# Gated DeltaNet layer: block inverses of two heads side by side, split weight buffers, last two scans in parallel

## The chip, the cores and the metric

The kernel runs on one NeuronCore of a Trainium2 chip. The metric is device time in microseconds (us) of one execution, the median of several runs. One execution is taken by the hardware profiler; its trace and page are what is quoted. Engines: PE is TensorE's matmul and PEld its weight load, DVE is VectorE, ACT is ScalarE, POOL is GpSimd, SP is SyncE, which issues the DMAs.

## The reference

A trunk of two pre-norm layers on 512 tokens of width 1024, float32: a gated DeltaNet layer, a squared-ReLU MLP (hidden width 4096), an HGRN2 layer, a second MLP and a last RMSNorm. The change lies in the first layer. With 8 heads of 128 and chunks, for each head:

```python
L = jnp.where(strict, jnp.einsum('nbhik,nbhjk->nbhij', kb, k) * decay, 0.0)
sol = lax.linalg.triangular_solve(L, rhs, left_side=True, lower=True, unit_diagonal=True)
...
def step(S, xs):
    v_new = u_c - jnp.einsum('bhck,bhkv->bhcv', w_c, S)
    o = jnp.einsum('bhck,bhkv->bhcv', qd, S) + jnp.einsum('bhij,bhjv->bhiv', a_c, v_new)
    S = S * dl[..., None, None] + jnp.einsum('bhck,bhcv->bhkv', kd, v_new)
```

The triangular system of each chunk is solved for every head; the recurrence over chunks (the scan) is then serial within a head. The head's output is normalised, multiplied by a gate and projected.

## The kernel before, in words

Activations lie with features on the 128 partitions and the 512 tokens along the free axis. Every projection in full precision is made of three products of rounded parts: a weight tile of 1024 x 256 is loaded as `raw` (L105), split into a high part `whi` by ScalarE (L111) and a low part `wlo` by VectorE (L112), each in two halves, and `project` (L122 to L124) issues for each of the 8 input blocks high x high, high x low and low x high, 128x512 each. A tile is a pair of 128-wide output blocks, 48 such products. `raw` has two buffers, `whi` and `wlo` three each.

In the DeltaNet layer (`gdn`, L269) a loop runs over j = 0 to 9. In step j the inputs of head j+1 are projected and convolved (`gdn_conv`), and, at a raised priority, the scan of head j-2 (`gdn_scan`), the local part of head j (`gdn_local`) and the block inverse of head j-1 (`gdn_inverse`) are issued; gate projections stand in steps 4, 6, 8 and 9 (`GATES`). The kernel uses chunks of 128 tokens, four in a head. A scheduler makes from the priorities and from the buffers one fixed order for each engine; the projections of later heads, of the gates and of the output projection fill TensorE between the small steps.

`gdn_inverse` inverts the four 128x128 unit triangular matrices of a head. It starts from 32x32 diagonal blocks, four blocks in each of four matrices, 16 products in a group, placed on the four diagonal 32x32 tiles of the array. For each of four levels:

- a group px (L499), ScalarE copies it to xd (L502);
- a group pu (L506), VectorE copies it into ud under a mask (L508) and transposes ud into wd (L509).

Then the 32-blocks are joined to 64 (px L516, pu L524 and L525) and the 64-blocks to 128 (px L536, pu L540). GpSimd copies ud to the diagonal of the result u (L511, four copies) and wd into w2 (L530, two copies), the operand of the 64x64 step. A float32 product runs in two passes, so a group of 16 products shows as x32 in the trace. A head has 12 such groups.

`gdn_scan` runs over the four chunks: pks (L559), r on VectorE, pw (L564), wv on VectorE, ps (L569), the new state s on VectorE, with the output po (L576, L578) beside it. The result is scaled by ScalarE into ot (L585, L591), transposed (pt, L594) and goes to VectorE. Then the gate is multiplied in and split into oh and ol, the inputs of the output projection (`out_proj`, L825), which starts with two weight tiles at once and goes through the heads in order; products with early heads stand on TensorE while the last scan runs.

PSUM: three buffers for projections, two with tag "ma" (local part and scan), three with tag "mb" (inverse).

Of the kernel before, what the change touches and what calls it, by code (L numbers as in the profile page):

```python
# [26 lines left out]
LINE, PAD = 2048, 352  # L27
LEVELS = (1, 2, 4, 8, 16)
HLEVELS = (2, 4, 8, 16, 32)
GATES = ((), (), (), (), (0,), (), (1,), (), (2,), (3,))  # L30


class Net:
    def __init__(self, tc, ctx, a):
        self.tc, self.nc, self.a = tc, tc.nc, a
        pool = lambda name, bufs=1, **kw: ctx.enter_context(tc.tile_pool(name=name, bufs=bufs, **kw))

        self.cp = pool("const")
        self.mp = pool("small")
# [6 lines left out]
        self.n = 0  # L46
        self.last_switch, self.since_switch = None, []
# [221 lines left out]
    def gdn(self, first):  # L269
# [23 lines left out]

        self.o, self.on = [None] * NH, [None] * NH
        hd = {0: self.gdn_conv(0, blocks)}
        self.gdn_silu([hd[0]])
        for j in range(NH + 2):
            todo = []
            if j + 1 < NH:
                hd[j + 1] = self.gdn_conv(j + 1, blocks)  # L300
                todo.append(hd[j + 1])
            sg = []
            for i in GATES[j]:
                sg += self.gdn_gates(i)
            with self.tc.high_priority(offset=3000):
                if j >= 2:
                    self.gdn_scan(j - 2, hd)
                if j < NH:
                    self.gdn_local(j, hd)
                if 1 <= j <= NH:  # L310
                    self.gdn_inverse(j - 1, hd)
                if todo or sg:
                    self.gdn_silu(todo, sg)
            for h, t in sg:
                self.gdn_gated(h, t)
        self.h = [self.load_x(c) for c in range(NB)]

# [54 lines left out]
    def gdn_conv(self, j, blocks):  # L372
        nc = self.nc
        kq = self.work("kq", [P, 2, T], bufs=4)
        v = self.work("v", bufs=4)
# [36 lines left out]
    def gdn_local(self, h, hd):  # L412
# [8 lines left out]
        ssk, ssq = self.work("ssk", [P, NC]), self.work("ssq", [P, NC], bufs=3)  # L421
        kd, e = self.work("kd", bufs=3), self.work("e")
# [13 lines left out]
        dd = self.work("dd", [P, NC], bufs=3)  # L436
# [23 lines left out]
        n, aa = self.work("n", bufs=2), self.work("aa", bufs=3)  # L460
# [14 lines left out]
    def gdn_inverse(self, h, hd):  # L475


        nc, mm, ident = self.nc, self.nc.tensor.matmul, self.ident
        n = hd[h][5].rearrange("p (c t) -> p c t", c=NC)
        blk = [slice(b, b + B) for b in range(0, P, B)]  # L480
        small = lambda name, bufs=1: self.work(name, [P, NC, B], bufs=bufs)
        psum = lambda name: self.mix(name, [P, NC, B], tag="mb")
        flat = lambda t: t.rearrange("p c t -> p (c t)")
        mask = lambda i: self.lmask[:, i].unsqueeze(1).to_broadcast([P, NC, B])
        uw = self.work("uw", [P, 2, T], bufs=2)
        u = uw[:, 0].rearrange("p (c t) -> p c t", c=NC)
        nc.gpsimd.memset(uw[:, 0], 0.0)
        ud, wd = small("ud"), small("wd")
        nc.gpsimd.tensor_copy(out=wd, in_=self.ident32.unsqueeze(1).to_broadcast([P, NC, B]))
        nt = small("xd")  # L490
        for b in blk:
            nc.vector.transpose(out=nt[b], in_=n[b, :, b])
        nc.vector.copy_predicated(out=wd, mask=mask(0), data=nt)
        nc.vector.transpose(out=flat(ud), in_=flat(wd))
        for i in range(1, len(LEVELS)):
            px = psum("px")
            for c in range(NC):
                for b in blk:
                    mm(px[b, c], lhsT=n[b, c, b], rhs=wd[b, c], start=True, stop=True,  # L499
                       tile_position=(b.start, b.start))  # L500
            x = small("xd")
            nc.scalar.copy(out=x, in_=px)  # L502
            pu = psum("pu")
            for c in range(NC):
                for b in blk:
                    mm(pu[b, c], lhsT=x[b, c], rhs=ud[b, c], start=True, stop=True,  # L506
                       tile_position=(b.start, b.start))
            nc.vector.copy_predicated(out=ud, mask=mask(i), data=pu)  # L508
            nc.vector.transpose(out=flat(wd), in_=flat(ud))  # L509
        for b in blk:  # L510
            nc.gpsimd.tensor_copy(out=u[b, :, b], in_=ud[b])  # L511

        px, x = psum("px"), small("xd")
        for c in range(NC):
            for l, r in (blk[0:2], blk[2:4]):
                mm(px[r, c], lhsT=n[l, c, r], rhs=wd[l, c], start=True, stop=True, tile_position=(l.start, r.start))  # L516
# [3 lines left out]
        l, r = blk[0], blk[1]  # L520
        w2 = uw[:, 1, 0:2 * B * NC].rearrange("p (c t) -> p c t", c=NC)
        for c in range(NC):
            for l, r in (blk[0:2], blk[2:4]):
                mm(pu[l, c], lhsT=x[r, c], rhs=ud[r, c], start=True, stop=True, tile_position=(r.start, l.start))  # L524
            mm(pu[blk[1], c], lhsT=ud[blk[1], c], rhs=x[blk[1], c], start=True, stop=True, tile_position=(B, B))  # L525
        for l, r in (blk[0:2], blk[2:4]):
            nc.vector.tensor_copy(out=u[l, :, r], in_=pu[l])
        nc.gpsimd.memset(w2[0:B, :, B:2 * B], 0.0)
        for i in (0, 1):
            nc.gpsimd.tensor_copy(out=w2[blk[i], :, i * B:(i + 1) * B], in_=wd[blk[i]])  # L530
        nc.vector.tensor_copy(out=w2[blk[1], :, 0:B], in_=pu[blk[1]])

        l, r = slice(0, 64), slice(64, P)
        px = self.mix("px", [P, NC, 2 * B], tag="mb")
        for c in range(NC):
            mm(px[r, c], lhsT=n[l, c, r], rhs=w2[l, c], start=True, stop=True, tile_position=(0, 64))  # L536
        nc.scalar.copy(out=w2[r], in_=px[r])
        pu = self.mix("pu", [P, NC, 2 * B], tag="mb")
        for c in range(NC):
            mm(pu[l, c], lhsT=w2[r, c], rhs=u[r, c, r], start=True, stop=True, tile_position=(64, 0))  # L540
        nc.vector.tensor_copy(out=u[l, :, r], in_=pu[l])
        uf = uw
        hd[h] = hd[h] + (uf,)

    def gdn_scan(self, h, hd):

        nc, mm, ident = self.nc, self.nc.tensor.matmul, self.ident
        kq, kd, vr, qd, aa, n, ssq, dd, uf = hd[h]
        k, u = kq[:, 0], uf[:, 0]
        ck = lambda t, c: t[:, c * P:(c + 1) * P]  # L550
        col = lambda n, c: self.col(n, c, h)
        po = self.mix("po", tag="ma")
        s = None
        for c in range(NC):
            if s is None:
                r = ck(vr, c)
            else:
                pks = self.mix("pks", [P, P], tag="ma")
                mm(pks, lhsT=ck(k, c), rhs=s, start=True, stop=True)  # L559
                r = self.work("r", [P, P], bufs=2)  # L560
                nc.vector.scalar_tensor_tensor(out=r, in0=pks, scalar=col("neg", c), in1=ck(vr, c),
                                               op0=ALU.mult, op1=ALU.add)
            pw = self.mix("pw", [P, P], tag="ma")
            mm(pw, lhsT=ck(u, c), rhs=r, start=True, stop=True)  # L564
            wv = self.work("wv", [P, P], bufs=2)
            nc.vector.tensor_scalar(out=wv, in0=pw, scalar1=dd[:, c:c + 1], scalar2=None, op0=ALU.mult)
            if c < NC - 1:
                ps = self.mix("ps", [P, P], tag="ma")
                mm(ps, lhsT=ck(kd, c), rhs=wv, start=True, stop=True)  # L569
                sn = self.work("s", [P, P], bufs=3)  # L570
# [11 lines left out]
        ot = uf[:, 1]  # L582
# [9 lines left out]
        pt = self.mix("pt", tag="ma")  # L592
# [419 lines left out]
```

## Time and profile before

| | |
|---|---|
| median of three runs | 1373.54 us (1373.2 to 1375.23) |
| the profiled execution's own time | 1373.13 us |
| its span, first to last instruction | 1371.0 us |
| granted TensorE clock | 0.997 |
| busy in 45 to 345 us: PE / DVE / ACT / POOL | 298.4 / 224.2 / 163.3 / 37.0 us |
| starts of the first px (L499) and of the last scan transpose (L594) | 62.3 to 342.6 us |

In the rows of the timeline stand the start in us from the span's start, the length in us, the engine, the line, the operation, output <- inputs, shapes and the count of instructions merged; in square brackets the engine's idle time before and what ended it. In the rows of groups: count, busy us, mean ns of one, idle time before. In the rows of waits: who waited for whom, us in total, times, longest. A row of windows has the busy us and the count of PE, PEld, DVE, ACT and POOL in that stretch, then the granted clock, the share of the DMA engines and GB/s. Matmuls are pipelined, so a row's length is longer than the distance to the next start.

### The profile page before, as it was taken

How to read it: one execution, taken by the hardware profiler on the slowest of the kernel's cores; microseconds unless marked ns; L12 is line 12 of the kernel's file. 1: busy time of each engine (PE TensorE's matmuls, PEld its weight loads, DVE VectorE, ACT ScalarE, POOL GpSimd, SP SyncE). 2: the span in 40 equal slices, each digit the busy share in tenths (PEclk: the TensorE clock that was granted, in tenths of full speed). 3: DMA queues.
4: the chain of work that ended last, by engine and by line, in shares of the span. 5: the costliest groups of instructions: out<-in, count | busy, mean ns of one | idle time of the engine just before them, and what ended most of it. 6: DMA issues, size and time to landing. Idle time of an engine off the chain costs nothing.

```text
span 1371.0 us, 24070 instructions
## 1 busy us (share of the span) xinstructions
PE 1351.2 (99%) x10084; PEld 1101.3 (80%) x10084; DVE 829.5 (61%) x1528; ACT 583.8 (43%) x1089; POOL 212.7 (16%) x232
## 2 busy tenths in 40 slices
PE   8999999999999999999999999999999999999997
PEld 5777777777888888888888788787788888888897
DVE  6998777764844444444473985769784444445453
ACT  5655555544434214233124666466533422314242
POOL 4011111110200120201221023031110021120232
PEclk9999999999999999999999999999999999999999
DMA  5131111122222232222221212121042222232232
GB/s 198 62 98 62 61 33 63 46 77 97 92 94 98 99 109 92 92 93 93 100 99 48 93 63 93 63 93 63 32 153 93 93 93 93 94 111 102 93 134 82
DMA packets 23501, 121.55 MB, mean 89 GB/s; under 512 B 3809, under 2 KB 7009, under 8 KB 9825
## 3 DMA queue, kind: packets, MB, share of 16 engines
q1 hardware_dynamic: 23392, 120.02, 24.8%
q8 instruction: 79, 1.29, 0.4%
q14 instruction: 30, 0.24, 0.1%
HBM read 117.91 MB, written 2.10 MB: 88 GB/s over the span
## 4 chain that ended last, share of the span: by engine, by line
PE 90%; DVE 4%; ACT 4%; issue 1%; DMA 1%; POOL 0%; SPq 0%; POOLq 0%; ACTq 0%; DVEq 0%
PE pj L122 25%; PE pj L123 25%; PE pj L124 25%; PE pga L464 1%; PE pu L506 1%; PE px L499 1%; PE gr L734 1%; ACT L91 1%; PE pw L564 1%; PE pj L680 1%; PE pj L679 1%; PE pj L678 1%; ACT whi L111 1%; PE po L576 1%; DVE ol L723 0%
## 5 line engine op out<-in xcount | busy, mean ns | idle before, releaser
L112 DVE TENSOR_TENSOR wlo<-raw,whi 128x1024 fp32r<-128x1024 f32 (+2 forms) x217 | 290.6, 1353 | 165.9 <-ACT whi L111 163.8
L111 ACT CAST whi<-raw 128x1024 fp32r<-128x1024 f32 (+2 forms) x222 | 221.8, 1023 | 390.1 <-PE pj L123 379.5
L122 PE MATMUL pj<-yh,whi 128*128 128x512 f32 x960 | 384.8, 401 | 0.7 <-ACT whi L111 0.7
L123 PE MATMUL pj<-yl,whi 128*128 128x512 f32 x960 | 383.5, 400 | 0.0
L124 PE MATMUL pj<-yh,wlo 128*128 128x512 f32 x960 | 382.2, 399 | 0.0
L122 PEld LDWEIGHTS pj<-yh,whi 128*128 128x128 f32 x960 | 181.4, 189 | 37.2 <-ACT whi L111 1.8
L123 PEld LDWEIGHTS pj<-yl,whi 128*128 128x128 f32 x960 | 181.5, 189 | 35.4
L124 PEld LDWEIGHTS pj<-yh,wlo 128*128 128x128 f32 x960 | 181.2, 189 | 35.4
L123 PE MATMUL pj<-ol,whi 128*128 128x512 f32 x336 | 131.3, 391 | 0.0
L872 DVE TENSOR_TENSOR gate<-pj,rB 128x512 f32<-128x512 f32 x56 | 38.6, 691 | 148.6 <-PE pj L124 148.6
L124 PE MATMUL pj<-oh,wlo 128*128 128x512 f32 x320 | 125.1, 391 | 0.0
L122 PE MATMUL pj<-oh,whi 128*128 128x512 f32 x320 | 124.9, 390 | 0.0
L874 POOL TENSOR_TENSOR kd<-kd,gate 128x512 f32<-128x512 f32 x18 | 23.3, 1293 | 462.2 <-DVE gate L872 462.2
L858 ACT ACTIVATE z<-pj 128x512 f32<-128x512 f32 x64 | 38.0, 594 | 113.6 <-PE pj L124 109.6
L123 PEld LDWEIGHTS pj<-ol,whi 128*128 128x128 f32 x336 | 63.1, 188 | 13.0
L124 PEld LDWEIGHTS pj<-oh,wlo 128*128 128x128 f32 x320 | 60.1, 188 | 12.2
L122 PEld LDWEIGHTS pj<-oh,whi 128*128 128x128 f32 x320 | 60.2, 188 | 12.1
L124 PE MATMUL pj<-kq,wlo 128*128 128x512 f32 (+1 forms) x192 | 68.3, 356 | 0.5 <-DVE wlo L112 0.5
L123 PE MATMUL pj<-kq,whi 128*128 128x512 f32 (+1 forms) x192 | 68.3, 356 | 0.0
L122 PE MATMUL pj<-kq,whi 128*128 128x512 f32 (+1 forms) x192 | 68.0, 356 | 0.0
L162 POOL TENSOR_TENSOR sqacc<-sqacc,z 128x512 f32<-128x512 f32 x25 | 37.4, 1496 | 119.0 <-ACT z L160 114.8
L91 ACT ACT_TABLE_LOAD x37 | 47.5, 1283 | 1.4 <-PEq L1004 0.7
(342 smaller groups left out, 2052.4 us busy)
## 6 DMA issues: line engine op xcount, KB each, us to landing
raw<-down SPq DMA_DIRECT2D x36, 1024.0 KB, 4.8
raw<-up SPq DMA_DIRECT2D x32, 1024.0 KB, 4.7
raw<-gdn_in SPq DMA_DIRECT2D x14, 1024.0 KB, 4.8
raw<-hgrn_fq SPq DMA_DIRECT2D x8, 1024.0 KB, 4.8
raw<-gdn_out SPq DMA_DIRECT2D x4, 1024.0 KB, 4.8
raw<-hgrn_i SPq DMA_DIRECT2D x4, 1024.0 KB, 4.8
raw<-hgrn_gate SPq DMA_DIRECT2D x4, 1024.0 KB, 4.6
raw<-hgrn_out SPq DMA_DIRECT2D x4, 1024.0 KB, 4.8
```

Source lines behind the costliest of these rows:

```text
L91: i = self.nc.scalar.preload_act_table_set(name)
L111: self.nc.scalar.copy(out=hi[:, k], in_=raw[:, k])
L112: eng.tensor_tensor(out=lo[:, k], in0=raw[:, k], in1=hi[:, k].bitcast(F32), op=ALU.subtract)
L122: mm(o, lhsT=hi[:, k, c], rhs=yh, start=(k == 0), stop=False)
L123: mm(o, lhsT=hi[:, k, c], rhs=yl, start=False, stop=False)
L124: mm(o, lhsT=lo[:, k, c], rhs=yh, start=False, stop=(k == NB - 1))
L162: e.tensor_tensor(out=self.sq, in0=self.sq, in1=t, op=ALU.add)
L464: mm(pga[:, c - c2], lhsT=ck(k, c), rhs=kq[:, :, c * P:(c + 1) * P], start=True, stop=True)
L499: mm(px[b, c], lhsT=n[b, c, b], rhs=wd[b, c], start=True, stop=True, tile_position=(b.start, b.start))
L858: nc.scalar.activation(out=z, in_=out, func=AF.Relu)
L872: nc.vector.tensor_tensor(out=t, in0=out, in1=self.r2b, op=ALU.mult)
L874: e.tensor_tensor(out=self.h[c], in0=self.h[c], in1=t, op=ALU.add)
```

## The change

- The inverse takes two heads at once, in steps j = 2, 4, 6 and 8. Each group of small products holds 32 products (both heads), each copy, masked copy and transpose is 256 columns wide instead of 128, except the first transposes (still one for each head and block) and the GpSimd copies to u (eight in a pair). `SCANS` places the scans: heads 0 to 5 in steps 3 to 8, heads 6 and 7 together in step 9.
- The third buffer of `whi` and `wlo` becomes a tile of its own (`whi3`, `wlo3`) that every third weight uses. In the DeltaNet layer the weights go without it, and the 16 KB per partition of the two hold one more buffer each for kq, v, kd, aa and n, and ot and w2 (`slot`, `extra`).
- The last scan uses "mb" in PSUM, its small tiles lie in a kq buffer and its ot in the n part of `wlo3`, so that it can run beside the scan of head 6.
- ssq and dd get five buffers; two constants for the placement in memory change.

```diff
+SCANS = ((), (), (), (0,), (1,), (2,), (3,), (4,), (5,), (6, 7))
...
     def weight_tiles(self):
-        return tile("raw", F32, 2), tile("whi", F32R, 3), tile("wlo", F32R, 3)
+        self.nw_tiles += 1
+        last = self.nw_tiles % 3 == 0 and not self.two
+        return (tile("raw", F32, 2), *(tile(t + "3", F32R, 1) if last else tile(t, F32R, 2) for t in ("whi", "wlo")))
...
+        self.two = True
+        xa, xb = (self.wp.tile([P, 4, T], F32, tag=t, bufs=1, name=self.name(t)) for t in ("whi3", "wlo3"))
+        self.extra = dict(kq=xa[:, 0:2], v=xa[:, 2], kd=xa[:, 3], aa=xb[:, 0], n=xb[:, 1], ot=xb[:, 2], w2=xb[:, 3])
...
-                if j >= 2:
-                    self.gdn_scan(j - 2, hd)
+                for i in SCANS[j]:
+                    self.gdn_scan(i, hd)
...
-                if 1 <= j <= NH:
-                    self.gdn_inverse(j - 1, hd)
+                if 2 <= j <= NH and j % 2 == 0:
+                    self.gdn_inverse((j - 2, j - 1), hd)
...
+    def slot(self, tag, h, n, shape=None):
+        return self.extra[tag] if h % n == n - 1 else self.work(tag, shape, bufs=n - 1)
...
             px = psum("px")
-            for c in range(NC):
+            for a, c in each:
                 for b in blk:
-                    mm(px[b, c], lhsT=n[b, c, b], rhs=wd[b, c], start=True, stop=True,
+                    mm(px[b, a, c], lhsT=n[a][b, c, b], rhs=wd[b, a, c], start=True, stop=True,
...
-            nc.vector.copy_predicated(out=ud, mask=mask(i), data=pu)
+            nc.vector.copy_predicated(out=m3(ud), mask=mask(i), data=m3(pu))
             nc.vector.transpose(out=flat(wd), in_=flat(ud))
-        for b in blk:
-            nc.gpsimd.tensor_copy(out=u[b, :, b], in_=ud[b])
+        for a in (0, 1):
+            for b in blk:
+                nc.gpsimd.tensor_copy(out=u[a][b, :, b], in_=ud[b, a])
...
-        w2 = uw[:, 1, 0:2 * B * NC].rearrange("p (c t) -> p c t", c=NC)
+        w2 = self.extra["w2"].rearrange("p (a c t) -> p a c t", a=2, c=NC)
...
+        last = h == NH - 1
+        tag = "mb" if last else "ma"
+        if last:
+            room = self.work("kq", [P, 2 * NC, P], bufs=4)
...
-        ot = uf[:, 1]
+        ot = self.extra["n" if last else "ot"]
```

The order on TensorE between two levels of an inverse, before: the last levels of head 7. A name's number tells tiles apart; L499 is px, L506 is pu, the others are a gate's projection and the transposes of head 6's scan.

```order
L506 MATMUL pu_4114<-ud_4009,xd_4112 32x32 x16
L122 MATMUL pj_4267<-yh_93,whi_4233 128x512
L123 MATMUL pj_4267<-yl_94,whi_4233 128x512
L124 MATMUL pj_4267<-yh_93,wlo_4234 128x512
L122 MATMUL pj_4267<-yh_107,whi_4233 128x512
L499 MATMUL px_4133<-wd_4010,n_3643 32x32 x16
L123 MATMUL pj_4267<-yl_108,whi_4233 128x512
```

After, between two levels of the pair of heads 6 and 7, with px now in L516 and pu in L523 (n_2879 and n_3421 are the two heads' matrices):

```order
L523 MATMUL pu_3694<-ud_3575,xd_3692 32x32 x32
L129 MATMUL pj_3970<-yh_146,wlo_3964 128x512
L127 MATMUL pj_3970<-yh_155,whi_3963 128x512
L128 MATMUL pj_3970<-yl_156,whi_3963 128x512
L129 MATMUL pj_3970<-yh_155,wlo_3964 128x512
L127 MATMUL pj_3970<-yh_170,whi_3963 128x512
L516 MATMUL px_3729<-wd_3576,n_2879 32x32 x16
L516 MATMUL px_3729<-wd_3576,n_3421 32x32 x16
L128 MATMUL pj_3970<-yl_171,whi_3963 128x512
```

Each group has become twice as long and stands once for two heads, with five projections in this gap instead of four.

GpSimd at the last inverse, before (head 7; L511 writes the diagonal of u, L530 writes w2):

```order
L489 COPY wd_4010<-ident_206 128x128
L487 MEMSET uw_4007 128x512
L528 MEMSET uw_4007 32x4x32
L472 TENSOR_TENSOR kq_2962<-x_3636,kq_2962 128x512
L511 COPY uw_4007<-ud_4009 32x4x32 x4
L530 COPY uw_4007<-wd_4010 32x4x32 x2
```

After (heads 6 and 7; w2 lies in the weight tile, so it is printed as wlo):

```order
L506 COPY wd_3576<-ident_206 128x256
L548 MEMSET wlo_68_467 32x8x32
L486 TENSOR_TENSOR kq_2577<-x_3414,kq_2577 128x512
L529 COPY uw_3573<-ud_3575 32x4x32 x8
L550 COPY wlo_68_467<-wd_3576 32x8x32 x2
```

Eight copies to u stand ahead of the two to w2, where four stood.

TensorE in the last scan, before (head 7; L564 is pw, L569 ps, L576 po, L559 pks, the rest is the output projection):

```order
L564 MATMUL pw_4308<-r_4306,uw_4007 128x128
L122 MATMUL pj_4419<-oh_2480,whi_4409 128x512
L123 MATMUL pj_4419<-ol_2481,whi_4409 128x512
L124 MATMUL pj_4419<-oh_2480,wlo_4410 128x512
L569 MATMUL ps_4312<-wv_4310,kd_3584 128x128
L576 MATMUL po_4294<-wv_4310,aa_3644 128x128
L578 MATMUL po_4294<-s_4301,kq_2962 128x128
```

After (heads 6 and 7; pw is L593, ps L598, po L605; the small tiles of head 7 lie in kq_4100):

```order
L593 MATMUL pw_4025<-v_2312,uw_3573 128x128
L593 MATMUL pw_4102<-v_2578,uw_3573 128x128
L127 MATMUL pj_4215<-oh_2307,whi_4206 128x512
L128 MATMUL pj_4215<-ol_2308,whi_4206 128x512
L598 MATMUL ps_4029<-wv_4027,kd_2820 128x128
L605 MATMUL po_4024<-wv_4027,aa_2880 128x128
L598 MATMUL ps_4105<-kq_4100,whi_67_466 128x128
L605 MATMUL po_4101<-kq_4100,wlo_68_467 128x128
L588 MATMUL pks_4034<-s_4031,kq_2311 128x128
```

The two scans' products alternate, and one or two projections stand between two steps of the same head instead of three.

More of the change, by code (lines that the diff above doesn't have):

```diff
@@ L46, in __init__ @@
         self.n = 0
+        self.nw_tiles, self.two = 0, False
         self.last_switch, self.since_switch = None, []
@@ L457, in gdn_local @@
         self.act(e, e, AF.Exp)
[L460 removed]
+        n, aa = self.slot("n", h, 3), self.slot("aa", h, 4)
         for c2 in range(0, NC, 2):
```

114 lines of the change are left out of this document (62 added, 52 removed).

## The prediction, made before the changed kernel ran

> **What bounds the kernel now.** I read the page first, then the windows of the stage that the change touches, then TensorE's waits there, and last its timeline instruction by instruction.
>
> ```profile
> span 1371.0 us, 24070 instructions
> PE 1351.2 (99%) x10084; PEld 1101.3 (80%) x10084; DVE 829.5 (61%) x1528; ACT 583.8 (43%) x1089; POOL 212.7 (16%) x232
> PE 90%; DVE 4%; ACT 4%; issue 1%; DMA 1%; POOL 0%; SPq 0%; POOLq 0%; ACTq 0%; DVEq 0%
> ```
>
> TensorE (PE) is busy all the time and carries 90% of the chain that ended last. The DeltaNet layer lies between about 45 and 345 us. Its window, and who made TensorE wait in it:
>
> ```profile
> 45.00:345.00 300.00, 298.40 (x3692) 228.90 (x3692) 224.17 (x603) 163.34 (x463) 37.02 (x75) 1.00 0.19 65
> PE pt L594 <- ACT uw L591: 0.5, 2, 0.3
> PE px L536 <- DVE uw L531: 0.4, 1, 0.4
> ```
>
> In 300 us TensorE waited 0.9 us for other engines, at a granted clock of 1.00. Whatever VectorE (224 us) and ScalarE (163 us) save there is hidden, and so is a small chain as long as projections stand between its steps. Only what shortens TensorE's own sequence pays, and only a wait that is not there today costs.
>
> So the question is what a group of small products costs TensorE beyond its arithmetic. The timeline of TensorE around two groups (x32 is 16 products, each in two passes):
>
> ```profile
> 169.50 0.45 PE L499 MATMUL px<-wd,n 32*32 32x32 f32 x32
> 169.89 0.50 PE L123 MATMUL pj<-yl,whi 128*128 128x512 f32 x1
> 170.22 0.39 PE L124 MATMUL pj<-yh,wlo 128*128 128x512 f32 x1
> 170.45 0.40 PE L122 MATMUL pj<-yh,whi 128*128 128x512 f32 x1
> 170.79 0.45 PE L506 MATMUL pu<-ud,xd 32*32 32x32 f32 x32
> 171.18 0.50 PE L123 MATMUL pj<-yl,whi 128*128 128x512 f32 x1
> 171.51 0.39 PE L124 MATMUL pj<-yh,wlo 128*128 128x512 f32 x1
> 171.74 0.39 PE L122 MATMUL pj<-yh,whi 128*128 128x512 f32 x1
> L499 PE MATMUL px<-wd,n 32*32 32x32 f32 x1024 | 16.5, 194 | 0.0
> ```
>
> Starts, not durations, are what counts in a pipelined engine. Two projection products follow each other at 0.23 us (170.22 to 170.45, 171.51 to 171.74). From the projection at 170.45 to the one at 171.51 it is 1.06 us with the group between; without it, two pitches, 0.46. The group costs 0.60 us. Of that its own streaming is little: its 32 records last 0.45 from first start to last end and one lasts 0.194, so 31 pitches take 0.26, 8.3 ns each, 0.27 for 32. The other 0.33 us is paid once a run: 0.11 going in (0.34 instead of 0.23), about 0.12 coming out, 0.10 at the first projection after it (0.33).
>
> **The change part by part.** The profiled execution took 1373.13 us with a span of 1371.0; the median of the runs is 1373.54. I subtract from the first and carry the 0.4 over.
>
> *Groups for two heads.* The number of products stays; the number of unbroken runs falls. Counted in the order of both programs up to the end of the DeltaNet layer, TensorE has 122 runs of 32x32 and 64x64 products before (96 groups, some split by other work) and 63 after (48 groups, some split). 59 runs fewer at 0.33 us are 19.5 us. This supposes that a run of 64 streams on as one of 32 does. The nearest row is a pair of groups of the second layer that stand back to back:
>
> ```profile
> 892.57 0.39 PE L122 MATMUL pj<-yh,whi 128*128 128x512 f32 x1
> 892.89 0.82 PE L734 MATMUL gr<-ol 128*32 128x32 f32 x64
> 893.64 0.50 PE L123 MATMUL pj<-yl,whi 128*128 128x512 f32 x1
> 893.97 0.39 PE L124 MATMUL pj<-yh,wlo 128*128 128x512 f32 x1
> ```
>
> From 892.57 to 893.97 it is 1.40 us; less 0.46 the 64 cost 0.94, where 0.60 + 0.27 = 0.87 was expected: 0.07 more. If all 48 merged groups pay that, 3.4 us go and 16.1 stay. Those two groups each had their own data to wait for, the merged ones have one wait; I take the middle, 17.8 us. [...]
>
> *Longer steps in the level chain.* Between px and pu lies a ScalarE copy, between pu and the next px a masked copy and a transpose on VectorE, now 256 instead of 128 columns wide.
>
> ```profile
> 168.02 0.45 PE L506 MATMUL pu<-ud,xd 32*32 32x32 f32 x32
> 168.55 0.30 DVE L508 COPY_PREDICATED ud<-lmask,pu 128x128 f32<-128x128 uint8 x1
> 168.89 0.31 DVE L509 STREAM_TRANSPOSE wd<-ud 128x128 f32<-128x128 f32 x1
> L502 ACT COPY xd<-px 128x128 f32<-128x128 f32 x32 | 8.5, 267 | 35.8 <-PE px L499 35.7
> L541 DVE COPY uw<-pu 64x256 f32<-64x256 f32 x8 | 3.3, 414 | 3.8 <-PE pu L540 3.7
> L681 ACT ACTIVATE uw<-pj,rsr 128x256 f32<-128x256 f32 x16 | 7.3, 469 | 9.2 <-PE pj L680 9.2
> ```
>
> The trace has no masked copy of 256 columns; a plain one takes 0.414, so I estimate 0.41 to 0.44 for each VectorE step (0.30 and 0.31 today, 0.2 to 0.27 more for both) and for the copy between 0.267 and 0.469, taken as 0.4 (0.13 more). The order answers with one more projection in each gap, 0.23 us: the tightest gap after pu holds five projections instead of four, that after px three instead of two. VectorE itself issues half as many steps, 10 us less work by these rows, hidden as said. What is left uncovered is between nothing and 0.2 us for each of the 48 groups; where TensorE waited 0.9 us in all today, I take 0.5 (bounds 0 and 10).
>
> *GpSimd's copies.* The diagonal blocks go to u in eight copies (L529) instead of four (L511), and the two w2 copies (twice as wide) stand behind them; px of the 64x64 step waits for w2.
>
> ```profile
> L511 POOL COPY uw<-ud x32: 280/292/1299, 83.9 to 320.2; 32x128 f32<-32x128 f32 x32
> 206.23 3.13 POOL L511 COPY uw<-ud 32x128 f32<-32x128 f32 x4 [19.01 <-DVE ud L508]
> 206.83 1.18 DVE L112 TENSOR_TENSOR wlo<-raw,whi 128x1024 fp32r<-128x1024 f32 x1
> L530 POOL COPY uw<-wd 32x128 f32<-32x128 f32 x16 | 4.6, 285 | 0.7
> ```
>
> At 0.292 the eight take 2.3 us and the w2 copies 0.6 to 0.9. In the bad case (four took 3.13 us beside a weight split on VectorE) it is 6.3 + 0.9 = 7.2, behind about 0.8 us from the last product of the last level's pu to the end of its masked copy. Counted in the order and taken at the pitches above, that product and px stand 6.2, 7.8, 9.6 and 5.0 us apart in the four pairs: no wait in the good case (4.0), 1.8 + 0.2 + 0 + 3.0 = 5.0 us in the bad one. I take 0.5. [...]
>
> *The last two scans side by side.* Each scan is a chain: pw, VectorE, ps, VectorE, pks, VectorE, pw.
>
> ```profile
> 330.47 0.39 PE L564 MATMUL pw<-r,uw 128*128 128x128 f32 x2
> 331.40 0.39 PE L569 MATMUL ps<-wv,kd 128*128 128x128 f32 x2
> 332.31 0.41 PE L559 MATMUL pks<-s,kq 128*128 128x128 f32 x2
> 333.25 0.40 PE L564 MATMUL pw<-r,uw 128*128 128x128 f32 x2
> L566 DVE TENSOR_SCALAR wv<-pw,dd 128x128 f32<-128x128 f32 x32 | 11.2, 349 | 8.7 <-PE pw L564 8.4
> ```
>
> A hop takes 0.91 to 0.94 us with two or three projections in it. Now the second scan's products and one or two projections fill it, about as long; but VectorE serves two steps of 0.349 in each hop. Bounds: nothing, or 0.35 + 0.35 more on each of ten hops, 7 us. VectorE has room for both in 0.9 us, so I take 0.8.
>
> *Weight buffers and queues.* Two buffers in the layer instead of three: a pair's split needs 2 x 1.02 + 2 x 1.35 = 4.8 us (rows below) and may start when the pair before the previous one is used up, a pair being 48 projections, 11 us by the pitch alone: cost nothing. Without that cover it would be up to 4.8 us a pair.
>
> ```profile
> L112 DVE TENSOR_TENSOR wlo<-raw,whi 128x1024 fp32r<-128x1024 f32 (+2 forms) x217 | 290.6, 1353 | 165.9 <-ACT whi L111 163.8
> L111 ACT CAST whi<-raw 128x1024 fp32r<-128x1024 f32 (+2 forms) x222 | 221.8, 1023 | 390.1 <-PE pj L123 379.5 <-DMA raw<-gdn_in 6.6 <-DMA raw<-hgrn_fq 2.2
> raw<-gdn_out SPq DMA_DIRECT2D x4, 1024.0 KB, 4.8
> ```
>
> The third weight of the output projection takes the buffer in which the last scan's result lies, so its low part comes after that scan's transposes. Behind these TensorE has 49 projections, 11 us, before it needs it; VectorE's queue up to there (the scan's result, two gates, two splits of each kind) is about 6 us: nothing. On SyncE two loads of x stand before the first gdn_out load and wait for buffers of head 4, whose scan ends 28 us of projections before that weight is used; the load lands in 4.8: nothing. Behind the middle of the output projection all five orders are the same.
>
> Sum: 17.8 - 0.5 - 0.5 - 0.8 = 16.0 us. 1373.1 - 16.0 = 1357.1, and against the median 1357.5.
>
> **The rivals.** *Half exposed:* the longer steps and the GpSimd copies show at the upper bounds of about half their terms (5 + 2.5 + 3.5 = 11 instead of 1.8): 17.8 - 11 = 6.8 us, 1366.7. For it: VectorE is 75% busy in the window, in order, with 1.35 us splits ahead of small steps. Against it: the same queue costs 0.9 us today.
>
> *The 0.33 us isn't a price of a run* but waiting of its first product for its data, which merging leaves. Then only chains are rearranged, and the time stays within 2.7 us. Against it: entering and leaving cost the same at every run shown, and the way out and the first projection after it wait for nothing.
>
> *Slower, a queue behind VectorE:* with both heads in one group nothing of these two heads goes on while the group's masked copy stands behind a weight split. It is one mechanism, in the 24 VectorE steps between pu and the next product: each behind one split (1.35 us) gives 32.4 - 17.8, 14.6 us slower, 1388. It decides from 17.8 / 24 = 0.74 us a step. For it: VectorE's in-order queue; against it: the order puts the steps where TensorE has 1.2 us or more of other work.
>
> **How the numbers follow.** Forecast (gain 12 to 21) 0.65; half exposed (3 to 12) 0.20; no gain 0.07; slower 0.08. A measurement of this kernel can tell 0.2%, 2.7 us, from no change (the three runs lie within 2.1 us). So faster 0.85, same 0.07, slower 0.08. The range goes from 19.5 and about 2 us more, if the fewer switches between projections and 128-wide products count too (a gain of 22, 1351.5), to a gain of 5.5 (1368): all of the forecast and most of the half-exposed case.
>
> **What would show it.** Right: the small products' lines keep their busy time or nearly, a group of 64 costs 0.87 to 0.94 us between projections, TensorE's waits in the layer stay under 3 us, and the last scan's transposes (341.6 us now) come about 16 us earlier, with the rest of the program as long as before. Wrong: TensorE waits for the masked copies or for GpSimd's w2 copies; a seam well over 0.07 us within the 64; or a later layer that changes length.

## The result, and the profile after

The changed kernel takes 1364.65 us, median of four runs (1363.33 to 1366.03), against 1373.6 for the kernel before: ratio 0.9933, 95% interval 0.9916 to 0.995, so 9.2 us faster by the ratio (the two medians lie 8.95 us apart). The forecast was 1357.5 us with a range from 1351.5 to 1368.0. The direction and the range hold, but 16.0 us were forecast, and the gain lies nearer to the rival "half exposed" (6.8) than to the forecast.

The page of the changed kernel, profiled execution 1365.81 us:

```profile
span 1363.7 us, 23897 instructions
PE 1338.5 (98%) x10084; PEld 1096.9 (80%) x10084; DVE 823.2 (60%) x1472; ACT 579.3 (42%) x1061; POOL 206.1 (15%) x212
PE 86%; DVE 6%; ACT 5%; issue 2%; DMA 0%; POOL 0%; SPq 0%; POOLq 0%; ACTq 0%; DVEq 0%
```

TensorE's share of the last chain fell from 90% to 86%, and "issue" rose from 1% to 2%. The window of the layer:

```profile
45.00:345.00 300.00, 294.36 (x3738) 231.86 (x3737) 224.45 (x562) 163.70 (x443) 30.82 (x57) 1.00 0.19 65
```

And the waits of TensorE in it:

```profile
PE pu L523 <- issue: 1.8, 2, 1.3
PE pga L478 <- DVE aa L482: 0.8, 1, 0.8
PE pt L623 <- ACT wlo L620: 0.6, 2, 0.5
PE pj L129 <- DVE wlo L117: 0.6, 1, 0.6
PE px L556 <- DVE wlo L551: 0.6, 2, 0.3
PE px L516 <- DVE wd L510: 0.2, 1, 0.2
```

Where TensorE waited 0.9 us in this stretch before, it waits 4.6 now, and 1.8 of that for "issue", in the middle of a group. The group itself costs about what was forecast. The timeline of TensorE around one of the merged groups (x64 is 32 products in two passes):

```profile
89.03 0.39 PE L128 MATMUL pj<-yl,whi 128*128 128x512 f32 x1
89.35 0.75 PE L516 MATMUL px<-wd,n 32*32 32x32 f32 x64
90.03 0.50 PE L129 MATMUL pj<-yh,wlo 128*128 128x512 f32 x1
90.37 0.39 PE L127 MATMUL pj<-yh,whi 128*128 128x512 f32 x1
```

From 89.03 to 90.37 it is 1.34 us; less two pitches, 0.46, the group costs 0.88 us, for two heads. One head's group cost 0.60. Over all groups that stand like this between projections, the median is 0.89 us for 13 merged ones and 0.58 for 21 of the kernel before, so a merge saves 0.27 us by the medians and 0.32 by these rows.

To see where the time went I took, for both kernels, every distance between two starts on TensorE and subtracted the usual distance for that pair of kinds (0.228 us from projection to projection, 0.33 into a small group, 0.12 out of one, 0.0085 inside it, and so on). What is left over I call waiting, and the rest TensorE's own work. This waiting is more than the rows of waits list: it holds the slips that are too short for a row, and the time lost at half clock. From about the 850th projection on, every start of the changed kernel lies 7.28 us earlier (the last one 1360.49 and 1353.20 us), so all of the difference arises before 345 us. Up to there:

```
                      waiting, us            own work against before, us
              0-40   40-120   120-345
before        12.1      3.0       8.9           0
changed       14.9      7.6      11.9         -17.6
```

TensorE's own work fell by 17.6 us, and 17.8 had been forecast for it. The usual distances hold the price of a run, so this split supposes it, and it depends on how the kinds are told apart: 57 runs fewer at the 0.27 us of the medians are 15.4 us. The experiments test the price apart. The waits rose by 10.3 us, and 1.8 had been forecast. These two profiled executions lie 7.3 us apart and the ratio gives 9.2; a longer start of the program in this execution would explain it (below), but the other executions have no trace.

### The profile page after: what moved, and what is told of

The parts are those of the page before. It is cut to its first block, busy times and chain, and to the rows that moved or that the text cites. A ratio compares the mean times of both kernels' runs of the same rounds, so it can differ in the third digit from the quotient of the medians.

```text
span 1363.7 us, 23897 instructions
## 1 busy us (share of the span) xinstructions
PE 1338.5 (98%) x10084; PEld 1096.9 (80%) x10084; DVE 823.2 (60%) x1472; ACT 579.3 (42%) x1061; POOL 206.1 (15%) x212
## 3 DMA queue, kind: packets, MB, share of 16 engines
q8 instruction: 79, 1.29, 0.4%
## 4 chain that ended last, share of the span: by engine, by line
PE 86%; DVE 6%; ACT 5%; issue 2%; DMA 0%; POOL 0%; SPq 0%; POOLq 0%; ACTq 0%; DVEq 0%
PE pj L127 25%; PE pj L128 25%; PE pj L129 24%; ACT L93 1%; PE gr L763 1%; PE pga L478 1%; PE pu L523 1%; ACT whi L116 1%; DVE wlo L117 1%; ACT v L87 1%; PE px L516 1%; PE pw L593 1%; PE pj L709 1%; PE pj L708 1%; PE pj L707 1%
```

## The experiments

All times are medians. The kernel before took 1373.6 to 1374.65 us beside them, and a ratio to it is taken against those neighbours. A difference to the changed kernel is one between medians of different rounds, in which the kernel before moved by 1 us; where it matters, the difference with each taken against the kernel before beside it stands in brackets.

**One head at a time again.** The pair loops of `gdn_inverse` get one head, `uw` and w2 are shared by halves; everything else stays.

```diff
-        each = [(a, c) for a in (0, 1) for c in range(NC)]
+        each = [(0, c) for c in range(NC)]
...
-                if 2 <= j <= NH and j % 2 == 0:
-                    self.gdn_inverse((j - 2, j - 1), hd)
+                if 1 <= j <= NH:
+                    self.gdn_inverse((j - 1,), hd)
```

> The changed kernel with one edit undone: each head's block inverse is done by itself again, one head a step, so that the small products come in about 122 unbroken groups instead of 63; the third weight buffers' room, the later scans and the last two scans in parallel stay. Theory (a run of small products has a price of about 0.3 us on TensorE, and nearly all of the gain is this): TensorE's own work grows by 17 to 18 us again and the waits that came with the change (about 7 us between 20 and 340 us) go away with it, so 1372 to 1376 us, 8 to 11 us slower than the changed kernel. First rival (the gain comes from the room or from the scans in parallel, not from the number of groups): 1364 to 1367 us. Second rival (the waits that ate the gain come from the other edits and stay): 1379 to 1384 us.

It took 1378.27 us, ratio to the kernel before 1.0029 (1.0021 to 1.0038). So doing two heads at once is worth 13.6 us (13.0), and all the other edits together cost 4.0 us. The first rival falls. The theory has the sign right and the size too small, since it let the waits go away with the pairs; the second rival, that the other edits carry waits of their own, is nearer, and its 1379 to 1384 is a little too much.

**The room alone.** From the same kernel the later and parallel scans are taken out too; what is left of the change is that the layer's weights go without their third buffers, that the tiles have new places, and that ssq and dd have five buffers.

```diff
-SCANS = ((), (), (), (0,), (1,), (2,), (3,), (4,), (5,), (6, 7))
+SCANS = ((), (), (0,), (1,), (2,), (3,), (4,), (5,), (6,), (7,))
...
-        last = h == NH - 1
+        last = False
```

> Each head's inverse by itself, each scan two steps behind its head and the last two scans one after the other, as in the kernel before: of the change only the room from the third weight buffers, with the tiles' new places, is left. The version with single inverses and the later, parallel scans took 1378.3 us, 4 us more than the kernel before. Theory (the later scans cost about 2.5 us of it, because VectorE's queue in the first steps makes TensorE wait, and the start of the program 1 to 2 us): 1374.5 to 1376.5 us. Rival (the room is what costs, since tiles in new places order VectorE's work anew): 1377.5 to 1379.5 us. Second rival (the room costs nothing, not even at the start): 1373.5 to 1374.5 us.

It took 1377.97 us, ratio 1.0026 (1.0016 to 1.0037): 3.8 us slower than the kernel before. The first rival's range holds: the room, with all that was left of the change, is what costs, and the later and parallel scans cost 0.3 us, which is nothing. Three things make it up in its trace, where the projections from the 850th on stand 5.2 us later than in the kernel before. TensorE goes through 126 unbroken runs of small products instead of 120, 6 x 0.33 = 2.0 us. The start of the program took 1.8 us longer in this execution (a granted clock of 0.83 between 20 and 40 us instead of 0.91, see below). And TensorE waits for VectorE at 58 to 61 us, 0.79 us for aa and 0.60 us for the low part of a weight, where the kernel before doesn't wait at all. In the kernel before, the split of the weight that is used there stands on VectorE ahead of the local part's masks:

```profile
52.45 1.19 DVE L112 TENSOR_TENSOR wlo<-raw,whi 128x1024 fp32r<-128x1024 f32 x1
57.40 1.02 PE L464 MATMUL pga<-kq 128*128 128x256 f32 x4
58.61 0.41 DVE L468 TENSOR_TENSOR aa<-pga,e 128x256 f32<-128x256 f32 x1
58.94 0.59 DVE L466 SCALAR_TENSOR_TENSOR n<-pga,nd,e 128x128 f32<-128x128 f32 x2
```

With the room alone it stands between the two halves of that part, seven microseconds later (59.76 instead of 52.45):

```profile
58.77 0.41 DVE L482 TENSOR_TENSOR aa<-pga,e 128x256 f32<-128x256 f32 x1
59.33 1.10 PE L478 MATMUL pga<-kq 128*128 128x256 f32 x4 [0.79 <-DVE aa L482]
59.76 1.22 DVE L117 TENSOR_TENSOR wlo<-raw,whi 128x1024 fp32r<-128x1024 f32 x1
60.90 0.60 DVE L480 SCALAR_TENSOR_TENSOR n<-pga,nd,e 128x128 f32<-128x128 f32 x2
61.03 0.50 PE L129 MATMUL pj<-yh,wlo 128*128 128x512 f32 x1 [0.60 <-DVE wlo L117]
```

The wait of 0.60 us is the moved split's. The wait for aa is not: aa is done before the split starts, and it comes hardly later than in the kernel before (58.77 and 58.61), which had issued the second half of pga at 57.40 without waiting for it. Why it must wait here was not found out. That the missing third buffer is what moved the split was not tried by itself either; the new places of the tiles came with it. Nor are these three a fixed price of the room: the version with one head at a time, which has it too, has 121 runs by the same count and more waiting in their place.

**A full-array product in the middle of each level group.** VectorE, ScalarE and GpSimd do what they did; only TensorE leaves the small tiles once more.

```diff
             for a, c in each:
+                if (a, c) == (1, 0):
+                    mm(px[:, 2, 0], lhsT=n[0][:, 0], rhs=wd[:, 0, 0], start=True, stop=True)
```

> The changed kernel with one product of the full array (128 rows, 32 columns, float32, its result unused) put between the two heads' halves of each of the 32 level groups, so that these groups are split into two runs while VectorE, ScalarE and GpSimd do what they did. Theory (the price is that of going into and out of the small tiles): each split costs the way in and the way out and the product itself, 0.12 + 0.20 us by the rows of the changed kernel, 32 x 0.32 = 10 us of TensorE work; what of it falls into waits that TensorE has anyway (some 3 us of the 7) is not seen, so 7 to 10 us slower than the changed kernel, 1372 to 1375 us. Rival (no price of a run): only the added product counts, 32 x 0.06 to 0.1 us = 2 to 3 us, so 1366 to 1368 us.

It took 1373.55 us, 8.9 more than the changed kernel (8.3), 0.28 us a split, the added product included. The theory holds, the rival (2 to 3 us) falls. A split group in its trace:

```profile
102.61 0.40 PE L129 MATMUL pj<-yh,wlo 128*128 128x512 f32 x1
102.94 0.45 PE L527 MATMUL pu<-ud,xd 32*32 32x32 f32 x32
103.32 0.41 PE L525 MATMUL pu<-xd,n 128*128 128x32 f32 x2
103.66 0.45 PE L527 MATMUL pu<-ud,xd 32*32 32x32 f32 x32
104.05 0.50 PE L127 MATMUL pj<-yh,whi 128*128 128x512 f32 x1
104.38 0.39 PE L128 MATMUL pj<-yl,whi 128*128 128x512 f32 x1
```

From 102.61 to 104.38, less 0.46, it costs 1.31 us instead of 0.88. So 32 splits add 13.8 us of TensorE's work by this row, and 8.9 are seen. In this kernel no group stops for "issue" any more (1.8 us); the rest was not followed up.

**Less work on VectorE.** Two of the four taps of the short convolution are left out, in the changed kernel and in the kernel before.

```diff
-            for s in (1, 2, 3):
+            for s in (1,):
```

> The changed kernel with two of the four taps of the short convolution left out (48 instructions of VectorE of about 0.7 us, 33 us of its 227 us in the first layer), which changes what is computed. Theory (VectorE, 18 to 19 of 20 us busy between 40 and 100 us, makes TensorE wait there and so eats a part of the gain): the waits between 40 and 340 us shrink by 3 to 6 us here and by 0 to 1 us in the kernel before with the same taps left out, so this one is 13 to 16 us faster than that one. Rival (the waits come from instruction fetch and from the longer groups themselves, not from VectorE): the distance between the two stays 9 to 10.5 us.

> The kernel before with the same two taps of the short convolution left out. Both theories expect 0 to 2 us less than the kernel before (its TensorE waits hardly at all in the first layer), 1371.5 to 1373.5 us; what they differ in is the distance of the changed kernel with these taps left out to this one: 13 to 16 us if VectorE eats a part of the gain, 9 to 10.5 us if not.

They took 1362.51 and 1377.32 us. The distance of 14.8 us is what the theory expected, but the way to it is not: the kernel before got 3.1 us slower with less work, which nobody expected. Its TensorE has 126 runs of small products instead of 120, so the scheduler, with other times on VectorE, broke up more groups: 2.0 us, and 1.3 us more waiting. The changed kernel had 7 runs more (70 instead of 63, 2.3 us) and 5.5 us less waiting; 4.2 of that lies between 40 and 120 us, where the two gaps at the wait for aa and at the wait for the split (0.95 us over the usual distance each, 1.9) and the long stop for "issue" (1.5) are gone. So VectorE's queue accounts for perhaps 2 us of the lost gain, those two gaps; the stop for "issue" is no wait for VectorE (below). As a clean test of VectorE it is spoilt by the new order, and that the distance fell into the theory's range is luck.

**The start of the program.** In the changed kernel the first matmul of the normaliser's sum (ps) stands behind the 51st projection matmul, before behind the 54th. A dependence puts it behind a chosen one:

```diff
+            if self.ahead:
+                self.after(m, self.pjs[self.ahead // 3 - 1])
```

> The changed kernel with the first matmul of the normaliser's sum (ps) put back behind the 54th projection matmul, where it stands in the kernel before; the scheduler had put it behind the 51st. Theory (those three projections, 0.7 us, are what makes TensorE's wait there 5.2 to 5.5 us instead of 3.7 to 3.9, and the longer wait brings a second stretch of 3.4 us at half clock): the wait falls below 4.6 us, the stretch at half clock to 3.4 us, and the program gets 1.5 to 3 us shorter than the changed kernel, 1361.5 to 1363.5 us, without its spread of 2.5 us between executions. Rival (the start of the program is late because its loads land later, whatever TensorE's order): 1364 to 1366 us, with the half clock as long as before.

> The same with that matmul behind the 72nd projection matmul, so that the 18 products of two blocks of y, ready by 21 us, run in the gap. Theory (the gap is only an order's doing): TensorE's wait there falls under 1 us and the clock stays whole; of the 5.2 us of waiting and 3.4 us lost at half clock 3 to 7 us come back, 1358 to 1362 us, if the next weights are there in time. Rival (the next weights, split at about 31 us, bound the start anyway): TensorE waits for them instead, and the time stays within 1 us of the 54 version.

With 54 it took 1365.58 us: no gain. With 72 it took 1359.79 us, ratio to the kernel before 0.989 (0.9875 to 0.9905), 4.9 us less than the changed kernel (5.9) and the fastest version here. The wait for ps in the kernel before, and its stretch from 20 to 40 us:

```profile
PE ps L192 <- ACT one L254: 3.9, 1, 3.9
```

```profile
20.00:40.00 20.00, 16.11 (x67) 11.67 (x67) 10.48 (x19) 5.19 (x10) 3.85 (x4) 0.91 0.38 139
```

The same two rows of the changed kernel:

```profile
PE ps L197 <- ACT one L259: 5.2, 1, 5.2
```

```profile
20.00:40.00 20.00, 15.29 (x57) 10.89 (x58) 10.09 (x17) 4.65 (x10) 4.25 (x5) 0.83 0.32 113
```

And of the version with 72 (the one with 54 waits 4.7 us, at the same 0.83):

```profile
PE ps L197 <- DVE z L194: 0.6, 1, 0.6
```

```profile
20.00:40.00 20.00, 19.09 (x88) 13.64 (x87) 14.79 (x33) 9.29 (x20) 4.06 (x4) 1.00 0.46 163
```

The column behind POOL's is the granted clock. The trace of the kernel before has 3.41 us at half clock there, as the 0.91 gives it, (1 - 0.91) x 20 / 0.5 = 3.6; that of the changed kernel has 6.83, twice as much (0.83: 6.8). With three projections more the wait is still 4.7 us and the clock still 0.83, and the theory of the 54 falls; 21 of them close the gap. The loss at the start can't be put down to the change alone either: the clocks of the single executions lie between 0.994 and 0.997 in the kernel before (its 27 runs beside the first four experiments) and at 0.994 and 0.996 in the changed one. The profiled execution of the kernel before lost 1.7 us at half clock, that of the changed kernel 3.4: a difference of 1.7 us, about what the two traces lie closer together than the ratio says.

So the same edit was made to the kernel before:

> The kernel before with its normaliser's first matmul behind the 72nd projection matmul, as in the version of the changed kernel that had it there (1359.8 us). Theory (the start of the program is a loss of its own that the change made 1 to 3 us larger, and the rest of the difference lies in the first layer): this one is 1369 to 1371.5 us, so that the distance between the two with the gap closed is 9.5 to 12 us. Rival (the change costs nothing at the start): 1368 to 1369 us, a distance of 8.5 to 9.5 us as without it.

It took 1369.63 us, 9.8 us more than the changed kernel with the same edit (10.6 when each is taken against the kernel before beside it). The theory's range for the distance holds, 9.5 to 12, by little: with the gap closed in both, the change is worth about 10 us, and the missing 6 lie in the layer. Some of them lie there only in this version. The order of the changed kernel with 72 has no projection left to cover the transposes of the last scans:

```profile
324.36 1.10 PE L627 MATMUL pt<-ident,wlo 128*128 128x128 f32 x4
327.17 0.33 PE L627 MATMUL pt<-ident,wlo 128*128 128x128 f32 x1 [1.71 <-ACT wlo L624]
320.00:345.00 25.00, 23.18 (x102) 18.53 (x101) 17.44 (x40) 16.62 (x44) 4.85 (x3) 0.93 0.17 55
```

TensorE waits 1.7 us there for ScalarE, and the clock of 0.93 in this window is some 3.4 us at half clock, (1 - 0.93) x 25 / 0.5 = 3.5, which costs another 1.7. Neither the changed kernel without the dependence nor the kernel before with it has the like (clock 1.00 in the same window). The version of the last experiment below, which has the 72 too, shows the same. So by these traces some 3.4 us of what the start gained are lost again at the other end of the layer, and the distance of 9.8 would be up to 3.4 larger without that; it was not tried.

**The scans one after the other.** The last scan goes back to the buffers of the other scans (`last = False`), with `SCANS` as changed.

> The changed kernel with the last two scans on the same buffers again, so that the second follows the first. Theory (the twin scans saved about 0.8 us, since projections of the last gates stand ahead of them): 0 to 2 us slower than the changed kernel, 1364.5 to 1367 us. Rival (the scans in parallel carry a good part of the gain): 4 to 8 us slower, with TensorE's waits for VectorE in the scans of 3 us or more after 300 us.

It took 1376.67 us, 12.0 more than the changed kernel (11.0): outside both expectations. Up to the 800th projection its trace is no slower than the changed kernel's, and then the last scan stands bare, with no projections left to cover it:

```profile
338.56 0.49 PE L593 MATMUL pw<-r,uw 128*128 128x128 f32 x2 [0.44 <-DVE r L590]
344.05 1.25 PE L623 MATMUL pt<-ident,wlo 128*128 128x128 f32 x4 [3.85 <-ACT wlo L620]
```

Its windows there:

```profile
320.00:345.00 25.00, 19.68 (x109) 15.25 (x107) 7.79 (x28) 8.90 (x32) 0.00 (x0) 0.93 0.07 22
345.00:365.00 20.00, 17.51 (x70) 14.12 (x70) 18.02 (x29) 9.92 (x15) 4.86 (x3) 0.84 0.16 53
```

TensorE is busy 19.7 of 25 us, and the clock falls to half for 10 us, (1 - 0.93) x 25 / 0.5 + (1 - 0.84) x 20 / 0.5 = 9.9. The parallel scans don't gain anything over the kernel before; they pay for the later scans, which the pairs of heads need.

**The stops inside a group.** The page of the changed kernel counts 79 instruction transfers (q8, 1.29 MB, so 16 KB each) beside 20,168 matmul and weight-load records of TensorE, 255 to a transfer; I took them for the pieces of TensorE's program, some 256 instructions each. Both stops in the changed kernel end shortly after one has landed (1.44 and 1.29 us, see the table below). Small matmuls ahead of the first projection move the borders:

```diff
+        for _ in range(64):
+            nc.tensor.matmul(warm[:, 0:4], lhsT=zeros[:, 0:P], rhs=zeros[:, 0:4], start=True, stop=True)
```

> The changed kernel with 64 small matmuls more (128 x 4 columns on zeros, result unused) ahead of the first projection, while TensorE waits for its first data; they move every later instruction of TensorE by half of a 16 KB piece of its program. Theory (the two waits in the middle of a run of small products, 1.3 and 0.46 us, that end 1.44 and 1.29 us after the landing of such a piece, are waits for instructions): they go away or come at other runs, and the time changes by -2 to +1 us. Rival (they hang on those products or their data): they stay at the same runs with the same length.

It took 1383.37 us, since the 64 matmuls took 27.3 us and held the first projection until 31.3. The stop at the 281st and the one at the 750th projection (the 16 products of pab counted in) stayed, which looked like the rival. But each of these matmuls is two matmul and two weight-load instructions (the trace has 128 matmul records for the 64): 256 in all, a whole piece, and the borders fell where they had been. So once more with 32:

> The changed kernel with 32 small matmuls ahead of the first projection, 64 matmul and 64 weight-load instructions (the 64 of the earlier run made 256 instructions, a whole piece of 16 KB, so that the borders of the pieces fell on the same instructions again). The start gets some 5 to 8 us longer, which is not the point. Theory (the long waits inside a run are for pieces of the program): with the borders moved by half a piece they come at other runs than the ones at the 281st and 750th projection or vanish, and each one left ends 1.2 to 1.5 us after the landing of a piece. Rival (they hang on those products or their data): they stay at these two runs, 1.2 to 1.5 and 0.5 to 0.7 us long.

Its time, 1371.81 us, carries the longer start. Both stops are gone from their places, and there is one at another group, of 2.3 us, where the changed kernel had none. The changed kernel's long stop, and this kernel's:

```profile
102.90 0.59 PE L523 MATMUL pu<-ud,xd 32*32 32x32 f32 x44
104.79 0.38 PE L523 MATMUL pu<-ud,xd 32*32 32x32 f32 x20 [1.30 <-issue]
```

```profile
101.76 0.60 PE L518 MATMUL px<-wd,n 32*32 32x32 f32 x47
104.65 0.33 PE L518 MATMUL px<-wd,n 32*32 32x32 f32 x17 [2.29 <-issue]
```

The data of the group were there, since 44 and 47 of its 64 records had run. From the trace's transfers:

```
kernel, stop at projection   piece starts   lands    group goes on   after landing
changed, 281                    102.12     103.35       104.79           1.44
changed, 750                    294.14     295.07       296.36           1.29
32 matmuls, 278                 102.30     103.17       104.65           1.48
```

In the other kernels with pairs there are thirteen more such stops, of 0.5 to 1.5 us from start to start, and they end 1.2 to 1.5 us after a landing. In the kernel before, in the versions with one head at a time and in the one with split groups there is none over 0.3 us; the kernel before with two taps left out has one of 0.33. What settles it is where they stand in the program. Count TensorE's records in a trace (weight loads, matmuls and the few others) up to the first product behind a stop: in all sixteen, and in the one of 0.33, the count leaves 193 or 194 when it is divided by 256. In the changed kernel 1729 and 6594 records stand ahead, 6 and 25 whole pieces and 193 or 194 more; with the 64 matmuls it is 1985 at the 281st projection, one piece more; with 32 it is 1729 again, at another group. The theory holds: these are waits for instructions, by this count at one place of a piece, and the long groups bring them.

**GpSimd's w2 copies first.** On top of the version with 72, the memset and the two copies for w2 stand ahead of the eight copies into u.

```diff
+        nc.gpsimd.memset(w2[0:B, :, :, B:2 * B], 0.0)
+        for i in (0, 1):
+            nc.gpsimd.tensor_copy(out=w2[blk[i], :, :, i * B:(i + 1) * B], in_=wd[blk[i]])
         for a in (0, 1):
             for b in blk:
                 nc.gpsimd.tensor_copy(out=u[a][b, :, b], in_=ud[b, a])
```

> The changed kernel with the normaliser's matmul behind the 72nd projection matmul, and with GpSimd's memset and two copies for w2 ahead of its eight copies into u. Theory (what TensorE waits for at px of the 64x64 step, 0.6 to 0.8 us in all, is VectorE's copy into w2, and GpSimd's copies are done in time): within 1 us of the version with the 72 alone, 1359 to 1360.5 us. Rival (the eight copies hold w2 up, as the upper bound of the prediction had it): 2 to 4 us faster, 1355.5 to 1358 us.

It took 1360.0 us, 0.2 more than the version with 72 (1.0), so nothing was gained. Here the px of the 64x64 step still waits for VectorE's copy:

```profile
PE px L560 <- DVE wlo L555: 0.6, 2, 0.3
```

## Why the prediction was right in kind and 7 us off in size

- *Groups for two heads, 17.8 us:* right in kind, at most a little large. The runs of small products in the trace went from 120 to 63, a merged group costs 0.88 us (0.87 to 0.94 was forecast), and putting a run back costs 0.28 us. Own work fell by 17.6 us by the usual distances and by 15.4 by the medians of the groups, so up to 2.4 of the missing us may be a price of a run nearer 0.27 than 0.33. The seam of 0.07 us in each group, which gave the lower end of 16.1, would have shown as 0.94; it is hardly there.
- *Longer steps of the level chain, 0.5 us:* right that they are covered. The masked copy of 256 columns takes 0.445 us and the transpose 0.442 (0.41 to 0.44 was estimated), ScalarE's copy 0.374 (0.4). TensorE's waits list none of them; the 0.2 us at px L516 are for the first masked copy (L510), ahead of the levels.
- *GpSimd's copies, 0.5 us:* near in size by luck. TensorE never waits for GpSimd there; the step waits 0.6 us in all, for VectorE's copy into w2 (L551), which the prediction didn't look at. Moving GpSimd's copies gave nothing.
- *Twin scans, 0.8 us:* fits beside the kernel before (0.3, together with the later places of the scans). What I didn't see is how much hangs on them: without the second scan beside the first, 12 us are lost.
- *Weight buffers and queues, 0:* wrong, the first of two steps that failed. The room costs 3.8 us with one head at a time. I asked whether a weight could be split in time; what I didn't cost is that the split moves in VectorE's order (a wait of 0.60 us), and that the scheduler makes a new order when anything is moved (six more runs of small products, about 2 us, and a new wait for aa, 0.79 us). Which part of the room does this stays open.
- *Waits that weren't in the sum:* the second. For the merged groups by themselves 17.8 - 0.5 - 0.5 = 16.8 us were forecast, and 13.6 came. 2.0 us of the 3.2 that are missing are the two stops for instructions, by the trace; the rest is not told apart from the price of a run. Nothing in the kernel before shows such a stop, and the rival "half exposed" named VectorE and GpSimd for its loss.

From the kernel before to the changed one it is +3.8 for the room, +0.3 for the later and parallel scans and -13.6 for the pairs, -9.5 in all, with 9.2 measured. These are three steps of one chain, so that they add up is no proof of the parts; the 0.3 between 9.5 and 9.2 is the drift from round to round. The signs that I named for a right forecast came half true: the group's cost and the later layers' length as said, but the waits in the layer 4.6 us instead of under 3, and the last of the scan's transposes at 333.5 us instead of 342.6, 9 us earlier instead of 16.

## What to carry to other kernels

Where one engine is the bound and small groups of work interrupt its long ones, count the interruptions and price one from the starts in the timeline: merging them saves about that price each (0.33 us forecast, 0.27 to 0.32 measured here). But cost the room that the merging needs as an edit of its own, by asking what moves in each engine's order when a buffer goes, and expect to lose a few microseconds to a new order that nobody designed. And look for gaps that the scheduler leaves elsewhere: one dependence at the start of the program was worth 4.9 us, half as much as the whole change. Then look at the whole trace again: behind the gap that was closed here, a new one of 3.4 us opened at the end of the layer.

## What the runs showed of the hardware

- *The stops in the groups of 64 stand at one place of the program's pieces.* A group of 64 matmul records with their weight loads is 128 instructions in 0.75 us (the row at 89.35), half of what a piece of 16 KB holds by the count above. Sixteen stops of over 0.3 us inside such groups, over all the versions with pairs, end 1.2 to 1.5 us after a piece has landed, all with 193 or 194 records ahead of them beyond whole pieces of 256; in the layer of the changed kernel a piece takes 0.9 to 1.5 us to come. Of the 29 pieces that come in that layer two landed ahead of a stop; no version has more than three stops, and they cost 0.5 to 2.5 us each.
- *How long the clock was at half.* It was 3.41 us at the start of the kernel before and 6.83 at that of the changed one, and by the windows some 10 us (9.9) at the end of the layer with the scans one after the other. Projections start 0.43 us apart in it (24.56 to 24.99 in the kernel before) instead of 0.23. Behind waits for ps of 3.7 to 4.5 us (three kernels) the clock between 20 and 40 us was 0.91, behind waits of 4.6 to 5.5 us (six kernels) 0.83. In the version with 72 the window with the last scans' transposes (four from 324.36 on, 1.71 us of waiting, one at 327.17) has 0.93. The spread of some 2 us between executions of one and the same program would fit another 3.41 us at half clock, which cost 1.7; that is an estimate, only the profiled executions have a trace.
